# First stage by fourths with the modulation's chunks in front of products, and the heads' score halves in turn in two banks

## The chip, the cores and the metric

The kernel runs on one core of one Trainium2 chip. The metric is the device time of one execution in microseconds (us); lower is better. TensorE (PE) multiplies matrices into PSUM banks, VectorE (DVE), ScalarE (ACT) and GpSimd (POOL) work on elements, and SyncE (SP) issues most of the transfers from HBM. A measurement of this kernel tells about 1% from no change.

## What is computed

The program is two transformer blocks on 256 tokens of width 1024, all in float32. The first block has two layers, each with a modulation from a condition (adaln), differential attention, a pooling mixer, a convolution, an output product and a gated FFN of hidden width 2816. In layer 0 the 256 context tokens go the same way beside the 256 tokens of x, so 512 tokens are worked on; layer 1 needs only x (its keys still come from all 512). The second block (four mixing branches) is not touched. The parts that matter here, from the reference:

```python
def adaln(cond, w_mod, b_mod):
    m = jnp.dot(jax.nn.silu(cond), w_mod) + b_mod
    return jnp.split(m[..., None, :], 6, axis=-1)

# diff_attention, for each block of 128 queries; c = 0, 1 are the two halves of a head
        s = jnp.einsum('bhcqd,bhckd->bhcqk', q_blk, k_all).astype(jnp.float32) * scale
        p = jax.nn.softmax(s, axis=-1)
        a = p[:, :, 0] - lam * p[:, :, 1]
        return jnp.einsum('bhqk,bhkd->bhqd', a.astype(v_all.dtype), v_all)

# first_block, each layer
        sh1, sc1, g1, sh2, sc2, g2 = adaln(c, w_mod[l], b_mod[l])
        h = modulate(rms_norm(x, norm1_g[l]), sh1, sc1)
        q, k, v, up, ca, cb = project_inputs(h, w_in[l], q_norm_g[l], k_norm_g[l])
        attn = diff_attn_post(diff_attention(q, k_all, v_all, lam), subln_g[l], lambda_init)
        pool_o = pool_mixer(up, pool_w[l], pool_scale[l])
        conv_o = conformer_conv(ca, cb, conv_dw_w[l], conv_dw_b[l], conv_ln_g[l], conv_ln_b[l])
        mix = jnp.concatenate([attn, pool_o, conv_o], axis=-1)
        x = x + g1 * jnp.einsum('blm,md->bld', mix, w_out[l])
        x = x + g2 * swiglu(modulate(rms_norm(x, norm2_g[l]), sh2, sc2), w_ffn_in[l], w_ffn_out[l])
```

There are 4 heads, each with two halves of 64 rows for queries and keys and a value width of 128.

## The kernel before

Every large product is taken as three float32r matmuls (`mm3`, lines 359 to 361): both operands are split into a high part and a rest, and high by high, rest by high and high by rest are added in one bank. Features stand as `hH`, `hL` (high and rest). Weights come in chunks of 512 KB (`raw_chunk`, L337) on the SP queue into `wraw` (4 buffers); `weights` casts them on ACT to `whi` (L349) and takes the rest on DVE as `wlo` (L350). PSUM has 8 banks of 512 columns in four pools: `mm` 3, `md` 1, `sc` 2, `aux` 2. A tile scheduler puts each engine's instructions in a fixed order from the order of the code and what each waits for; buffers decide when a load may start.

**First stage.** The x columns come as two 1 MB transfers on ACT's queue, their squares are summed for the norm (L437, L441, L448, L452). The modulation's scale and shift for the first norm come in two groups of 8 chunks, each chunk one row block of 128 by 1024 columns, multiplied by the conditions in four column groups (`modulation`, L513, 256 columns each). When a group's 8 chunks are done, its sums are copied (L518), transposed by TensorE (L520) and added to a bias (L533); then `norm` makes the features of four of the eight row blocks (L495 on DVE, L497 hH on ACT, L498 hL on DVE). `first_norm(0)` runs ahead of any product. The second group's chunks are put between the products of the first three `ab` items (the convolution's inputs, each 8 row blocks by 512 tokens) by `feats` with the table `STEPS`, which gives how many chunks follow which product; the second half of the products waits for the second norm. The fourth item follows alone. The raw chunks share `wraw` and `wmod` buffers (two to one) with the weights of the products.

**What follows in layer 0.** Products for queries and keys, head norm and rope, values, then attention a head at a time among the products of the next head; taps of the convolution on DVE and POOL; the pooling; and last w_out.

**Attention.** A unit is one head and one block of 128 queries (`tt`): 256 keys for the context's blocks (tt < 2), 512 for the others; 16 units in layer 0, 8 in layer 1 in two blocks. `scores` does for each half c: a bank from `sc`, three matmuls on rows 64c to 64c+63, the maximum on DVE (L702), the exponential with its sum on ACT (L704). `values` takes the reciprocal and the difference (L711 to L713, DVE, in place in `e`), transposes it on TensorE (L716), copies it (L718, ACT, `aT`), multiplies by the values (L721), and scales the result (L725, L726). The loop issues the scores of one unit ahead of the values of the present one. `finish` norms a head (L732, L735), transposes it (L738) and splits it. The split pieces live in the pool `hid`, as tiles `hidH` and `hidL` of 512 columns.

**Other places touched.** `layer_scalars` (lam of the layer) and `decay` (a row of the second block) are small chains on ACT and DVE; before, both stand in the first layer's beginning as the scheduler finds room. `single` takes tiles of 512 columns from `hid` in the second block.

## Time and profile before

| | |
|---|---|
| median of 3 runs | 1404.02 us (1397.06 to 1407.89) |
| the profiled execution | 1406.04 us, its span 1404.2 us |
| mean granted clock of TensorE | 0.968 |
| TensorE busy | 1337.7 us, 95% of the span |
| DVE, ACT, POOL busy | 965.5, 602.9, 233.5 us (69%, 43%, 17%) |
| chain that ended last, by engine | PE 83%, DVE 6%, ACT 4%, DMA 3% |
| HBM read | 211.00 MB, 151 GB/s over the span |

A window row gives for a stretch how long each engine worked, how many instructions it had, and the mean granted clock (1.00 is 2.4 GHz, half of it 1.2 GHz). A timeline row gives the start, the length, the engine, the line and operation, what is written and read, and in brackets how long the engine had been idle before and what ended that. Matmuls overlap in the pipeline, so the step from one start to the next is a matmul's price, not the length shown. Times count from the span's start.

### The profile page before, as it was taken

The numbers are of one execution on the slowest core, as the hardware profiler recorded it, in microseconds if no ns is written. First come the engines' busy times: TensorE is split into PE (matmuls) and PEld (weight loads), VectorE is DVE, ScalarE is ACT, GpSimd is POOL, SyncE is SP. The second block draws the span as 40 slices with busy tenths as digits, with TensorE's granted clock in tenths as the row PEclk, the third lists the DMA queues.
The fourth block names the chain that finished last, engine by engine and source line by source line (L and its number), as shares of the span: only waits on it lengthen the run. The fifth ranks groups of instructions, "written<-read, shape, count | busy, mean of one in ns | idle before, by whom it ended". The sixth has DMA issues, their size and how long they took to land.

```text
span 1404.2 us, 22735 instructions
## 1 busy us (share of the span) xinstructions
PE 1337.7 (95%) x8754; PEld 1173.3 (84%) x8754; DVE 965.5 (69%) x1928; ACT 602.9 (43%) x1085; POOL 233.5 (17%) x274
## 2 busy tenths in 40 slices
PE   5899999899999999998988989999999999998999
PEld 2699667798888888888977879999977788998999
DVE  4599766678667767746976655555678677757565
ACT  3333454433222222335344544444565546656443
POOL 0056631310000000013316230000173002000000
PEclk9999999999999999998988889999999999999999
DMA  8424450425444667732321235555564423444553
GB/s 336 178 86 141 161 170 30 151 92 186 157 159 156 196 209 236 237 111 72 109 91 46 81 120 176 195 176 185 168 237 144 152 89 100 149 143 152 186 184 132
DMA packets 61309, 213.53 MB, mean 152 GB/s; under 512 B 6928, under 2 KB 8080, under 8 KB 60944
## 3 DMA queue, kind: packets, MB, share of 16 engines
q1 hardware_dynamic: 60768, 209.91, 44.8%
q10 hardware_dynamic: 432, 2.16, 0.4%
q8 instruction: 69, 1.13, 0.3%
q14 instruction: 40, 0.33, 0.1%
HBM read 211.00 MB, written 1.05 MB: 151 GB/s over the span
## 4 chain that ended last, share of the span: by engine, by line
PE 83%; DVE 6%; ACT 4%; DMA 3%; POOL 2%; issue 2%; SPq 0%; ACTq 0%; POOLq 0%; DVEq 0%
PE ps_mm L359 22%; PE ps_mm L360 22%; PE ps_mm L361 21%; PE ps_sc L359 2%; PE ps_aux L359 2%; DVE wlo L350 2%; PE ps_aux L361 2%; PE ps_aux L360 2%; PE ps_aux L721 1%; PE ps_sc L360 1%; PE ps_sc L361 1%; DVE cacc L820 1%; ACT whi L349 1%; PE ps_md L513 1%; DMA wraw<-in_w_dram 1%
## 5 line engine op out<-in xcount | busy, mean ns | idle before, releaser
L349 ACT CAST whi<-wraw 128x1024 fp32r<-128x1024 f32 (+2 forms) x292 | 300.5, 1033 | 528.6 <-PE ps_mm L360 257.4
L350 DVE TENSOR_TENSOR wlo<-wraw,whi 128x1024 fp32r<-128x1024 f32 (+2 forms) x296 | 356.5, 1206 | 163.4 <-ACT whi L349 160.9
L359 PE MATMUL ps_mm<-hH,whi 128*128 128x256 f32 (+1 forms) x1056 | 344.3, 329 | 11.1 <-ACT hH L497 8.9
L360 PE MATMUL ps_mm<-hL,whi 128*128 128x256 f32 (+1 forms) x1056 | 342.6, 326 | 2.2 <-DVE hL L498 2.2
L361 PE MATMUL ps_mm<-hH,wlo 128*128 128x256 f32 (+1 forms) x1056 | 342.6, 326 | 1.3 <-DVE wlo L350 1.3
L359 PEld LDWEIGHTS ps_mm<-hH,whi 128*128 128x128 f32 x1056 | 204.4, 195 | 32.4 <-ACT hH L497 10.7
L360 PEld LDWEIGHTS ps_mm<-hL,whi 128*128 128x128 f32 x1056 | 204.9, 194 | 19.6 <-DVE hL L498 3.8
L361 PEld LDWEIGHTS ps_mm<-hH,wlo 128*128 128x128 f32 x1056 | 204.6, 194 | 17.7 <-DVE wlo L350 2.5
L359 PE MATMUL ps_mm<-hidH,whi 128*128 128x256 f32 (+1 forms) x683 | 214.1, 316 | 1.7 <-ACT hidH L355 1.7
L360 PE MATMUL ps_mm<-hidL,whi 128*128 128x256 f32 (+1 forms) x683 | 214.4, 315 | 0.0
L361 PE MATMUL ps_mm<-hidH,wlo 128*128 128x256 f32 (+1 forms) x683 | 213.4, 314 | 0.0
L360 PE MATMUL ps_mm<-wlo,hH 128*128 128x256 f32 (+2 forms) x464 | 143.2, 310 | 3.5 <-DVE wlo L350 3.5
L359 PE MATMUL ps_mm<-whi,hH 128*128 128x256 f32 (+2 forms) x464 | 139.9, 310 | 2.1 <-ACT tm L647 1.4
L361 PE MATMUL ps_mm<-whi,hL 128*128 128x256 f32 (+2 forms) x464 | 141.9, 307 | 0.0
L359 PEld LDWEIGHTS ps_mm<-hidH,whi 128*128 128x128 f32 x683 | 129.2, 190 | 10.5 <-ACT hidH L355 1.9
L360 PEld LDWEIGHTS ps_mm<-hidL,whi 128*128 128x128 f32 x683 | 129.8, 190 | 8.9 <-issue 0.5
L361 PEld LDWEIGHTS ps_mm<-hidH,wlo 128*128 128x128 f32 x683 | 129.4, 190 | 8.0
L470 POOL TENSOR_TENSOR squares<-squares,scr 128x256 f32<-128x256 f32 (+1 forms) x28 | 31.6, 1130 | 561.3 <-ACT scr L469 560.8
L580 DVE CUSTOM_DVE_ANT_0 ps_md<-wmod,tm 128x512 f32<-128x512 f32 x160 | 111.5, 697 | 12.4 <-DMA wmod<-in_w_dram 9.7
L848 DVE SCALAR_TENSOR_TENSOR xT<-ps_mm,modv,xT 128x256 f32<-128x256 f32 x116 | 52.5, 479 | 74.1 <-PE ps_mm L361 74.1
L364 POOL TENSOR_TENSOR st<-st,mhalf 128x4 f32<-128x4 f32 (+3 forms) x54 | 65.1, 1209 | 198.8 <-DVE st L632 86.7
L360 PEld LDWEIGHTS ps_mm<-wlo,hH 128*128 128x128 f32 x464 | 88.3, 191 | 9.6 <-DVE wlo L350 5.8
(347 smaller groups left out, 1996.6 us busy)
## 6 DMA issues: line engine op xcount, KB each, us to landing
wraw<-in_w_dram SPq DMA_DIRECT2D x271, 512.0 KB, 3.3
wmod<-in_w_dram SPq DMA_DIRECT2D x85, 512.0 KB, 4.1
wraw<-in_w_dram SPq DMA_DIRECT2D x32, 448.0 KB, 3.2
xT<-in_x_dram ACTq DMA_DIRECT2D x2, 1024.0 KB, 7.0
single<-in_w_dram SPq DMA_DIRECT2D x8, 256.0 KB, 7.5
wraw<-in_w_dram SPq DMA_DIRECT2D x4, 288.0 KB, 3.5
tm<-in_rows_dram SPq DMA_DIRECT2D x4, 256.0 KB, 6.1
out_dram<-scr SPq DMA_DIRECT2D x8, 128.0 KB, 1.7
```

The source lines that it names most:

```text
L349: act.copy(out=hi[:, :m], in_=t[:, :m])
L350: P["split"] = dve.tensor_tensor(lo[:, :m], t[:, :m], hi[:, :m].bitcast(F32), op=ALU.subtract)
L359: pe.matmul(ps, a[0], b[0], start=start, stop=False)
L360: pe.matmul(ps, a[0], b[1], start=False, stop=False)
L361: P["product"] = pe.matmul(ps, a[1], b[0], start=False, stop=stop)
L364: pool.tensor_tensor(t, t, mhalf[:, :n], op=ALU.pow)
L470: eng.tensor_tensor(squares[:, lo:hi], squares[:, lo:hi], q, op=ALU.add)
L513: inst = pe.matmul(ps[g * 32:g * 32 + 32, :256], csil[:, k, :], t[:, g * 256:g * 256 + 256], start=(k == 0), stop=(k == KD - 1), tile_posi ...
L580: dve.tensor_tensor_reduce(bank("md"), t[:, i * 512:i * 512 + 512], crow[2 * j + i], 1.0, 0.0, ALU.mult, ALU.add, sums[j][:, i * KD + d:i ...
L721: pe.matmul(po[:, :128], aT[:, i * 128:i * 128 + 128], v[i][:, h * 128:h * 128 + 128], start=(i == 0), stop=(i == nk // 128 - 1))
L820: dve.scalar_tensor_tensor(av, u[:, j, :n, i:i + 256], colt[:, o + i:o + i + 1], av, op0=ALU.mult, op1=ALU.add)
L848: dve.scalar_tensor_tensor(xT[:, d, r], ps[:, s * 256 - lo:s * 256 - lo + 256], M(l, which, 1 - s)[:, d:d + 1], xT[:, d, r], op0=ALU.mult, ...
```

## The change

1. The modulation of the first norm comes in fourths (`first_modulation`): each fourth gives the scale and shift of two row blocks from four chunks of two row blocks by 512 columns, with matmuls of 128 columns (L515 in the new file). The weights of the ab items come by fourths too, 2 row blocks by the columns of all four items, so that `first_products` fills four banks (3 `mm`, 1 `sc`) a fourth at a time. The raw chunks go into 16 buffers of `hid` and `wmod`. `tc.issue_after` sets the chunks of the next fourth ahead of products.
2. x comes in four transfers of 512 KB at the head of the SP queue.
3. Attention: six score matmuls alternate between the halves, so between rows 0 to 63 and 64 to 127, into both `sc` banks; the maxima and exponentials come after both. Scores run two units ahead, and the product with the values (`values`) one unit late, apart from the transposes (`turned`, the first half of what `values` was).
4. `hid` has tiles of 1024 columns that hold high part and rest (`slot`, `single`); `feats` loses its interleaving; `layer_scalars` is issued after the first stage's products, `decay` late in layer 1's FFN.

```diff
...
@@ -33,13 +33,11 @@
 ROWS_PER_STEP = (3, 1)
 AHEAD = (2, 0)
 POOL_AFTER = ((14, 15), (5, 6))
-STEPS = {1: 1, 2: 1, 3: 1, 4: 1, 5: 1, 6: 1, 7: 1, 8: 1, 11: 9}
 NSCR = 4
 NXS = 3
 
 
-
-MOD_GROUPS = {0: ((4, 5, 0, 1), (6, 7, 2, 3)) + tuple(tuple(range(4 * i, 4 * i + 4)) for i in (2, 4, 3))}
+MOD_GROUPS = {0: tuple(tuple(range(4 * i, 4 * i + 4)) for i in (2, 4, 3))}
 
 
 MIX_PARTS = ((0, 1, 4, 5), (6, 7, 2, 3))
@@ -65,6 +63,12 @@
             cols = np.concatenate([np.arange(c * 256, c * 256 + 256) for c in parts])
             for k in range(8):
                 rows(("mod", l, g, k), "w_mod", (l,), cols, k * 128, 1)
+        if l == 0:
+            for q in range(4):
+                cols = np.arange(q * 256, q * 256 + 256)
+                for k in range(0, 8, 2):
+                    rows(("first", q, k), "w_mod", (l,), np.concatenate([D + cols, cols]), k * 128, 2)
+                rows(("abq", q), "w_in", (l,), np.arange(1792, 2304), q * 256, 2)
         for which in range(6):
             if (l, which) in BY_ROWS:
                 for d in range(8):
...
@@ -296,8 +300,8 @@
     colt = const.tile([128, NCOLS], F32, name="colt")
     dma.dma_start(out=colt[:, :NCOL0], in_=cols[:, :NCOL0])
     xT = const.tile([128, KD, 512], F32, name="xT")
-    for k in range(0, KD, 4):
-        act.dma_start(out=xT[:, k:k + 4], in_=xin.rearrange("p (k t) -> p k t", k=KD)[:, k:k + 4])
+    for k in range(0, KD, 2):
+        dma.dma_start(out=xT[:, k:k + 2], in_=xin.rearrange("p (k t) -> p k t", k=KD)[:, k:k + 2])
     first = const.tile([128, CST0], F32, name="first")
     act.dma_start(out=first, in_=cst[:, 0:CST0])
     ident = first[:, 0:128]
@@ -333,21 +337,28 @@
 
     def raw_chunk(key, pl="wraw"):
         kt, n = PLAN[key][4], len(PLAN[key][3])
-        t = (P["wmod"] if pl == "wmod" else wraw).tile([128, CHUNK], F32, name=pl)
+        t = (wraw if pl == "wraw" else P[pl]).tile([128, CHUNK], F32, name="raw" if pl == "hid" else pl, tag=pl)
         P["load"] = dma.dma_start(out=t[:, :kt * n], in_=w[INDEX[key], :, :kt * n])
...
...
...
@@ -503,6 +502,32 @@
     pool.memset(csil, 0.0)
     act.activation(csil[:, :, 0:2], C("c").rearrange("p (k j) -> p k j", j=2), AF.Silu)
     modv = {l: const.tile([128, 6, KD, 2], F32, name=f"modv{l}") for l in range(DEPTH)}
+
+    def first_modulation(q, pools, p):
+
+        ps = bank(p)
+        for k in range(0, KD, 2):
+            t = raw_chunk(("first", q, k), next(pools))[0]
+            P["first"] = P["load"]
+            for i in range(2):
+                for g in range(4):
+                    o = i * 512 + g * 128
+                    inst = pe.matmul(ps[g * 32:g * 32 + 32, :128], csil[:, k + i, :], t[:, o:o + 128],
+                                     start=(k + i == 0), stop=(k + i == KD - 1), tile_position=(0, g * 32))
+            yield inst
+        cp = P["wk"].tile([128, 256], F32, name="cp")[:, :128]
+        act.copy(out=cp, in_=ps[:, :128])
+        pe.transpose(ps[:, 256:384], cp, ident)
+        got = ps[:, 256:384].rearrange("p (w k c) -> p w k c", w=2, k=2)
+        r = slice(2 * q, 2 * q + 2)
+        for i, which in enumerate((1, 0)):
+            o = COLS["bmod0"][0] + which * 8 + 2 * q
+            dve.tensor_tensor(modv[0][:, which, r], got[:, i, :, 0:2],
+                              colt[:, o:o + 2].unsqueeze(2).to_broadcast([128, 2, 2]), op=ALU.add)
+            if which:
+                dve.scalar_tensor_tensor(scale1[0][:, :, r].rearrange("p j k -> p k j"), modv[0][:, 1, r], 1.0,
+                                         C("n1g")[:, r].unsqueeze(2).to_broadcast([128, 2, 2]),
+                                         op0=ALU.add, op1=ALU.mult)
 
     def modulation(l, group, pools=repeat("wmod"), p="md"):
 
...
@@ -690,23 +716,31 @@
         q0 = qts[0]
 
         def scores(j, tt):
+
             nk = 256 if tt < 2 else 512
             mx, s = st(2), st(2)
+            ps = [bank("sc"), bank("sc")]
+            qs = slice((tt - q0) * 128, (tt - q0) * 128 + 128)
+            for i, (a, b) in enumerate(((0, 0), (0, 1), (1, 0))):
+                for c in range(2):
+                    r = slice(c * 64, c * 64 + 64)
+                    with tc.issue_after(P["product"].ins) if i or c else nullcontext():
+                        P["product"] = pe.matmul(ps[c][:, :nk], qT[j][a][r, qs], kT[j][b][r, :nk], start=i == 0,
+                                                 stop=i == 2)
+            for c in range(2):
+                dve.tensor_reduce(mx[:, c:c + 1], ps[c][:, :nk], axis=AX.X, op=ALU.max, negate=True)
+            return nk, ps, mx, s
+
+        def exps(nk, ps, mx, s):
             e = []
             for c in range(2):
-                r = slice(c * 64, c * 64 + 64)
-                ps = bank("sc")
-                qs = slice((tt - q0) * 128, (tt - q0) * 128 + 128)
-                mm3(ps[:, :nk], (qT[j][0][r, qs], qT[j][1][r, qs]), (kT[j][0][r, :nk], kT[j][1][r, :nk]),
-                    True, True)
-                dve.tensor_reduce(mx[:, c:c + 1], ps[:, :nk], axis=AX.X, op=ALU.max, negate=True)
                 x = P["wk"].tile([128, 512], F32, name="e", bufs=4)
-                act.activation(x[:, :nk], ps[:, :nk], AF.Exp, bias=mx[:, c:c + 1], accum_out=s[:, c:c + 1])
+                act.activation(x[:, :nk], ps[c][:, :nk], AF.Exp, bias=mx[:, c:c + 1], accum_out=s[:, c:c + 1])
                 e.append(x)
             return nk, s, e
 
-        def values(j, tt, ss, nk, s, e):
-            h = h0 + j
+        def turned(j, tt, nk, s, e):
+
             r, cc = st(2), st(1)
             dve.reciprocal(r, s)
             dve.scalar_tensor_tensor(cc, s[:, 0:1], r[:, 1:2], lam, op0=ALU.mult, op1=ALU.mult)
...
@@ -742,15 +780,21 @@
 
         units = [(j, tt) for j in range(len(qT)) for tt in qts]
         sums = {j: st(4) for j in range(len(qT))}
-        ahead = scores(*units[0])
-        for i, (j, tt) in enumerate(units):
-            now = ahead
-            if i + 1 < len(units):
-                ahead = scores(*units[i + 1])
-            values(j, tt, sums[j], *now)
-            if tt == qts[-1]:
-                finish(j, sums[j])
-            each()
+        n = len(units)
+        held = {i: exps(*scores(*units[i])) for i in range(min(2, n))}
+        turn = {}
+        for i in range(n + 1):
+            ahead = scores(*units[i + 2]) if i + 2 < n else None
+            if i:
+                j, tt = units[i - 1]
+                values(j, tt, sums[j], *turn.pop(i - 1))
+                if tt == qts[-1]:
+                    finish(j, sums[j])
+            if i < n:
+                turn[i] = turned(*units[i], *held.pop(i))
+                if ahead:
+                    held[i + 2] = exps(*ahead)
+                each()
 
     def pooled(l, j, h, seqs, mix):
 
@@ -857,14 +901,39 @@
     row = rows_of_rstd(0, 512)
     h = new_h()
 
-    pools = cycle(("wraw", "wraw", "wmod"))
-
-    def first_norm(half):
-
-        yield from modulation(0, half, pools, "sc")
-        norm(h, 0, 512, parts(0, 0, scale1, (0, 1)), range(half * 4, half * 4 + 4), row, True)
-    for _ in first_norm(0):
-        pass
+    def first_products(items):
+
+        pools = iter(("hid",) * 9 + ("wmod",) * 2 + ("hid",) * 5)
+        ps = [bank("mm" if i < 3 else "sc") for i in range(4)]
+        mods = [first_modulation(q, pools, ("md", "sc")[q % 2]) for q in range(4)]
+        ws = {0: weights(("abq", 0))}
+
+        def first_norm(q):
+            for _ in mods[q]:
+                pass
+            norm(h, 0, 512, parts(0, 0, scale1, (0, 1)), range(2 * q, 2 * q + 2), row, True)
+
+        first_norm(0)
+        for q in range(4):
+            for k in range(2):
+                chunk = None
+                if q < 3 and k < 2 - min(q, 1):
+                    with tc.issue_after(P["product"].ins) if q or k else nullcontext():
+                        for _ in range(4 if q else 2):
+                            chunk = next(mods[q + 1])
+                    if q or k:
+                        P["behind"] = P["normed"], P["rest"]
+                        ws[q + 1] = weights(("abq", q + 1))
+                if k and q < 3:
+                    first_norm(q + 1)
+                wH, wL = ws[q]
+                with tc.issue_after(chunk.ins) if chunk else nullcontext():
+                    for (key, _), t in zip(items, ps):
+                        c = slice(key[2] * 128, key[2] * 128 + 128)
+                        mm3(t, (wH[:, k, c], wL[:, k, c]), tuple(x[:, 2 * q + k] for x in h), q + k == 0, q + k == 4)
+        P["behind"] = P["normed"], P["rest"], P["first"]
+        for (_, evac), t in zip(items, ps):
+            evac(t)
 
     def project_rows(l, d_list, make, ks, which, final, first_half, lo, after, each=None):
 
@@ -930,16 +999,17 @@
         n = 512 - lo
         qts = range(2 * seqs[0], 4)
         if not last:
-            queue.extend(modulation(0, g) for g in range(2, 5))
+            queue.extend(modulation(0, g) for g in range(3))
         mix = {}
         u, items = conv_inputs(l, h, seqs)
         if l == 0:
-            feats(items[:3], h, [(0, 512)], first_norm(1))
-            items = items[3:]
-            with tc.issue_after(P["load"].ins):
+            first_products(items)
+            items = []
+            with tc.issue_after(P["first"].ins):
                 R, K = open_consts(False)
                 dma.dma_start(out=colt[:, NCOL0:], in_=cols[:, NCOL0:])
-        layer_scalars(l)
+        with tc.issue_after(P["normed"].ins), tc.issue_after(P["rest"].ins), tc.issue_after(P["product"].ins):
+            layer_scalars(l)
         for it in items:
             feats([it], h, [(lo, 512)])
         acc, taps = conv_taps(l, u, seqs)
@@ -1041,7 +1111,8 @@
                 items = []
                 rows_step(0)
                 if last and f == 10:
-                    decay()
+                    with tc.issue_after(P["high"].ins), tc.issue_after(P["split"].ins):
+                        decay()
             final = t == 2
             if final:
                 h_next = new_h()
...
```

How the rows stand. On TensorE, at the start of the program, before the change (`ps_sc` is the bank of the modulation's sums, `csil` the condition, L437 the sums of squares, L452 the spread of the norm):

```order
L437 MATMUL ps_aux<-ones,scr 128x1
L513 MATMUL ps_sc<-wmod,csil 32x256 x4
L513 MATMUL ps_sc<-wraw,csil 32x256 x8
L513 MATMUL ps_sc<-wmod,csil 32x256 x4
L452 MATMUL ps_aux<-scr,ones 128x512
L513 MATMUL ps_sc<-wraw,csil 32x256 x8
L513 MATMUL ps_sc<-wmod,csil 32x256 x4
L520 MATMUL ps_sc<-first,cp 128x128 x2
L359 MATMUL ps_mm<-hH,whi 128x512
L513 MATMUL ps_sc<-wraw,csil 32x256 x4
L360 MATMUL ps_mm<-hL,whi 128x512
```

In the change the same place on TensorE (L515 is the modulation, L370 to L372 are the three matmuls of a product):

```order
L436 MATMUL ps_aux<-ones,scr 128x1
L515 MATMUL ps_md<-raw,csil 32x128 x24
L451 MATMUL ps_aux<-scr,ones 128x512
L515 MATMUL ps_md<-raw,csil 32x128 x8
L515 MATMUL ps_sc<-raw,csil 32x128 x16
L520 MATMUL ps_md<-first,cp 128x128
L370 MATMUL ps_mm<-hH,whi 128x512 x3
L370 MATMUL ps_sc<-hH,whi 128x512
L371 MATMUL ps_mm<-hL,whi 128x512
L372 MATMUL ps_mm<-hH,wlo 128x512
```

Four chunks stand ahead of the first transpose's sums as before eight of half the rows did, two chunks of the next fourth stand between those and the transpose, and the first products of all four items follow at once.

On TensorE at the first attention block of layer 1, before the change (L716 is the transpose of `e`, `ps_sc` the score banks):

```order
L359 MATMUL ps_sc<-hidH 128x512
L360 MATMUL ps_sc<-hidL,hidH 128x512
L361 MATMUL ps_sc<-hidH,hidL 128x512
L716 MATMUL ps_aux<-first,e 128x128 x4
L359 MATMUL ps_sc<-hidH 128x512
L360 MATMUL ps_sc<-hidL,hidH 128x512
L361 MATMUL ps_sc<-hidH,hidL 128x512
L721 MATMUL ps_aux<-tm,aT 128x128 x4
```

And in the change, the whole block:

```order
L728 MATMUL ps_sc<-hid 128x512 x18
L750 MATMUL ps_aux<-first,e 128x128 x4
L728 MATMUL ps_sc<-hid 128x512
L759 MATMUL ps_aux<-tm,aT 128x128 x4
L728 MATMUL ps_sc<-hid 128x512 x5
L750 MATMUL ps_aux<-first,e 128x128 x4
L759 MATMUL ps_aux<-tm,aT 128x128 x4
```

The scores of three units now stand ahead of the first transpose. DVE's order in the same block of the change (L731 is the maximum, L745 to L747 the reciprocal and the difference, L764 the scaled result):

```order
L731 TENSOR_REDUCE st_6472<-ps_sc 128x1 x2
L731 TENSOR_REDUCE st_6488<-ps_sc 128x1 x2
L731 TENSOR_REDUCE st_6504<-ps_sc 128x1
L745 RECIPROCAL st_6516<-st_6473 128x2
L731 TENSOR_REDUCE st_6504<-ps_sc 128x1
L746 SCALAR_TENSOR_TENSOR st_6517<-st_6473,st_6516,lam 128x1
L747 SCALAR_TENSOR_TENSOR e<-e,st_6517 128x512
```

The difference of the first unit (L747) stands behind both maxima of the third, where before the maxima of at most the next unit stood ahead of it.

## Rows read from the trace of the kernel before

**Rows 1.** Windows: stretch, length, busy PE PEld DVE ACT POOL, PEclk, DMA share, GB/s.
```profile
0.00:66.00 66.00, 44.71 (x250) 27.84 (x251) 31.86 (x87) 24.05 (x43) 3.97 (x16) 0.92 0.70 265
66.00:127.00 61.00, 61.00 (x514) 60.12 (x516) 60.97 (x103) 23.24 (x49) 31.03 (x26) 1.00 0.26 88
127.00:170.00 43.00, 42.27 (x305) 31.43 (x294) 36.36 (x78) 20.04 (x56) 31.01 (x50) 1.00 0.55 196
170.00:222.00 52.00, 48.30 (x299) 29.48 (x298) 32.94 (x81) 27.06 (x79) 14.67 (x17) 0.90 0.38 122
720.00:738.00 18.00, 13.94 (x57) 10.10 (x57) 11.09 (x27) 10.65 (x32) 1.07 (x1) 0.72 0.17 56
759.00:790.00 31.00, 27.94 (x131) 21.04 (x132) 16.72 (x40) 14.61 (x38) 9.78 (x13) 0.75 0.05 19
```

**Rows 2.** Timeline of the first stage, all engines, up to the first product.
```profile
22.65 0.44 PE L520 MATMUL ps_sc<-first,cp 128*128 128x128 f32 x2
...
26.33 1.65 DVE L495 SCALAR_TENSOR_TENSOR tm<-xT,scale,ps_aux 128x256 f32<-128x256 f32 x4
...
27.80 0.79 PE L359 MATMUL ps_mm<-hH,whi 128*128 128x512 f32 x1 [4.71 <-ACT hH L497]
```

**Rows 3.** Timeline of TensorE among the first products.
```profile
32.56 0.63 PE L359 MATMUL ps_mm<-hH,whi 128*128 128x512 f32 x1
32.99 0.63 PE L360 MATMUL ps_mm<-hL,whi 128*128 128x512 f32 x1
...
37.85 0.39 PE L359 MATMUL ps_mm<-hH,whi 128*128 128x512 f32 x1
...
38.30 0.39 PE L361 MATMUL ps_mm<-hH,wlo 128*128 128x512 f32 x1
38.62 0.64 PE L513 MATMUL ps_sc<-wraw,csil 128*32 128x256 f32 x8
...
39.52 0.39 PE L360 MATMUL ps_mm<-hL,whi 128*128 128x512 f32 x1
...
47.29 0.73 PE L359 MATMUL ps_mm<-hH,whi 128*128 128x512 f32 x2 [0.76 <-ACT hH L497]
```

**Rows 4.** Waits of the SP queue in 0:60 (us in total, times, longest us).
```profile
SPq L337 <- PE ps_sc L513: 12.7, 10, 4.8
```

**Rows 5.** Timeline of TensorE at score matmuls, in three places.
```profile
132.49 0.28 PE L361 MATMUL ps_mm<-whi,hL 128*128 128x256 f32 x1
132.70 0.49 PE L359 MATMUL ps_sc<-hidH 64*128 64x512 f32 x1
...
133.59 0.38 PE L359 MATMUL ps_mm<-whi,hH 128*128 128x256 f32 x1
...
210.68 0.50 PE L359 MATMUL ps_sc<-hidH 64*128 64x512 f32 x1
...
213.93 0.50 PE L359 MATMUL ps_sc<-hidH 64*128 64x512 f32 x1
...
717.83 0.50 PE L359 MATMUL ps_sc<-hidH 64*128 64x512 f32 x2
718.17 0.40 PE L360 MATMUL ps_sc<-hidL,hidH 64*128 64x512 f32 x2
```

**Rows 6.** Groups by line: count, busy us, mean ns, idle before (127:222; loads: whole).
```profile
L702 DVE TENSOR_REDUCE st<-ps_sc 128x1 f32<-128x512 f32 x16 | 11.0, 687 | 10.0 <-PE ps_sc L361 10.0
L713 DVE SCALAR_TENSOR_TENSOR e<-e,st 128x512 f32<-128x512 f32 x7 | 6.3, 896 | 0.1
L704 ACT ACTIVATE e<-ps_sc,st 128x512 f32<-128x512 f32 x16 | 11.1, 694 | 4.6 <-DVE st L702 2.9 <-DVE st L711 1.6
L704 ACT ACTIVATION_READ_ACCUMULATOR e<-ps_sc,st 128x1 f32 x30 | 6.1, 202 | 0.0
L704 ACT ACT_TABLE_LOAD x2 | 2.6, 1283 | 0.0
```

**Rows 7.** Waits of TensorE in 717:790 (us in total, times, longest us).
```profile
PE ps_sc L359 <- ACT e L704: 3.2, 2, 2.4
```

59 lines of the change are left out of this document (31 added, 28 removed).

## The prediction

> **What bounds the kernel now.** I read the windows of the stages first, then the timeline of each stage that the change touches, then the waits of the engines there. The windows [rows 1] say that TensorE sets the time nearly everywhere, and that the touched stages are where it does not. In 0:66 it works for 44.71 of 66 us, at a mean granted clock of 0.92. In 66:127 and 127:170 it is full (61.00 of 61, 42.27 of 43), and DVE is just as full in 66:127 (60.97). In 170:222 it has 48.30 of 52 at clock 0.90. The two attention blocks of layer 1, 720:738 and 759:790, are the loosest: 13.94 of 18 and 27.94 of 31, at clocks 0.72 and 0.75. So a microsecond that the first stage gives back should reach the end if what follows is full, and a matmul saved in 66:170 is worth its own time. In 170:222 and in layer 1's blocks the chain scores, maximum, exponential, transpose counts.
>
> In the first stage the timeline [rows 2, 3] shows the first product at 27.80, behind an idle 4.71 us for hH. The chunks of the second half of the modulation stand between products, and TensorE waits again at 47.29 when the second half's features come. The SP queue waits for buffers ten times, 12.7 us, until an L513 has read one [rows 4]. In 0:66 the DMA brings 265 GB/s at a share of 0.70 [rows 1]; that is 265/0.70 = 379 GB/s while it flows.
>
> **The first stage.** The bytes are the same, 12 MB of x, modulation and ab weights. Only their order changes, and 16 chunk buffers instead of a few keep the queue from waiting.
>
> *First product.* Ahead of the first transpose on TensorE stand 2 MB of x, 0.5 MB of ab weights, the 2 MB of fourth 0 and, by the order of TensorE shown above, the first 1 MB of fourth 1: 5.5 MB, 5.5/0.379 = 14.5 us, and 3 us that I allow for the start of the transfers: 17.5. The last chunk's matmuls and the copy of the sums bring the transpose to about 19.3. Before, from transpose (22.65) to product (27.80) took 5.15 us, of which 3.7 passed until the first features' tm at 26.33, since late weights' wlo stood ahead of it on DVE [rows 2]. In the change the ab weights of fourth 0 come first and are long split, so only about 2.5 us remain: first product 21.8, between 20 and 23.5.
>
> *Products.* 4 banks by 8 k by 3 is 96 matmuls. At full clock they start 0.225 us apart (37.85 to 38.30 is two) [rows 3], 22.1 us with 0.23 each. At the low clock they start 0.43 apart (32.56 to 32.99). I let 16 of them run so, 16 x 0.20 = 3.2 us; the bounds are 6 (1.2) and 24 (4.8).
>
> *Chunks between products.* From 38.30 to 39.52 there lie two product steps and one chunk of 8 matmuls of 256 columns: 1.22 - 0.45 = 0.77 us [rows 3]. Ten of the twelve chunks of fourths 1 to 3 stand behind the first product. Their matmuls are as many but half as wide; no row shows that width, so a chunk lies between 0.4 (half) and 1.0 (0.77 with a wait for data); I take 0.7 because the switches and the starts stay: 7 us.
>
> *Seams.* Before, one seam cost 0.76 us for hH at 47.29 [rows 3] and more for hL. Now there are three, 1.0 each: 3 us, between 1.5 and 6.
>
> 21.8 + 22.1 + 3.2 + 7 + 3 = 57.1 us, where the stage now ends 0.4 ahead of the window's end, at 65.6: **8.5 us gained**, with bounds, not all at once on one side, of 3 to 13. That DVE is full from 66 on [rows 1] does not take the gain away at once: its queue there is fed by the evacuations of these products and moves with them.
>
> *layer_scalars* and *decay* are costed at nothing. decay is a table load and some DVE operations on a few columns. It leaves the first stage (DVE 31.86 of 66 busy) [rows 1] for layer 1's FFN, where TensorE has products to cover it. A table load is 1.28 us [rows 6]; with as much again for DVE, 2.5 us is its price without that cover.
>
> **The attention of layer 0.** One half alone among products takes from 132.49 to 133.59, less one product step of 0.12: 0.98 us for three matmuls of 512, of which the product and score switches are about 0.3 [rows 5]. Two halves cost about 2.0. In the change six matmuls stand next to each other with alternating rows. That two of them can run side by side is seen at 717.83: a pair L359 and a pair L360 start only 0.34 us apart, the time of one [rows 5]. If that holds for all three pairs a unit costs about 1.1, if not 6 x 0.23 + 0.4 = 1.8. It saves 0.2 to 0.9 for 512 keys and half that for 256. Eight of the sixteen units lie in 127:170, where TensorE is full: at most 4 x 0.9 + 4 x 0.45 = 5.4, at least 1.2; **I take 4**, since the trace shows the pair.
>
> In 170:222 the units are not hidden. There they come 3.25 us apart now (210.68, 213.93) [rows 5]. In the change both banks are taken at once, so scores (0.9), the first maximum (0.69) and both exponentials (2 x 0.89 with their accumulator reads) follow each other until both banks are free [rows 6]: 3.4, with handovers 3.6. That is 0.35 more for each of some five such units; with less matmul time in between I book **+1.5**, between -4 and +5.
>
> **Layer 1.** Here the whole loop is exposed. In 720:738 TensorE waits 3.2 us in two pieces for an exponential to free a score bank [rows 7]. In the change three units' scores (18 matmuls) stand ahead of the first transpose, and DVE has the third unit's maximum in front of the first unit's L747, as its order shows. Four units at the 3.6 from above are 14.4, and behind the last exponential come its L747 (0.90) [rows 6], transpose, copy and values with handovers, some 4 in all: about 18.5 us, as now. The second block has up products and transposes between; two units ahead should fill part of its 3 us of waiting: **-2 for both**, between -7 and +3. The order shows two more table loads than before on ACT, 2 x 1.28 us [rows 6], beside products; they and the slightly shifted second half are booked at 0, within 3 either way.
>
> **Sum.** -8.5 - 4 + 1.5 - 2 = -13. Against the profiled execution (1406.0) that is 1393, against the median of the three runs (1404.0) 1391: **1392**.
>
> **A rule weighed.** The pair at 717.83 speaks for side by side work [rows 5]. The Trainium skill, page "TensorEngine Tiling (Array Packing)", section "PSUM Bottleneck", says that tiling makes TensorE faster but not the emptying of PSUM, which may then be the limit. The 3.2 us of TensorE waiting for an exponential [rows 7] agree with it. By that rule the 4 us in layer 0 would be lost too, and the sum would be -9; if the loop grew as well it is the third rival.
>
> **Rivals.**
> 1. *Both parts work fully.* Chunks cost 0.5, products run at full clock (stage ends near 52, -13), pairs overlap everywhere (-8 in layer 0, -4 in layer 1): -25, 1380. For it speaks the pair at 717.83; against it that the clock falls whenever TensorE idles in a stage (0.72 in 720:738) [rows 1].
> 2. *The first stage's gain is swallowed.* DVE is as full as TensorE in 66:127 [rows 1]. If what it does there (wlo, taps) is bound by loads or by work that cannot start earlier, the 8.5 us turn into waits there, and only the attention is left: -3, 1402. Against it: in 66:127 the DMA runs at a share of 0.26 only, so loads do not hold it.
> 3. *The attention loop gets longer*, which ends on the other side. Both banks are taken together, and L747 (0.90) stands behind the maxima of the unit two ahead. If each exposed unit pays both, 0.35 + 0.90 = 1.25 us, the seven of layer 0's last stretch and eight of layer 1 cost 19; with -8.5 of the first stage that is +10: 1416. It decides against the change from 8.5/15 = 0.6 us a unit. Against it: DVE has slack there: ahead of the maxima of 512 keys it idles 10.0 us in all, waiting for scores [rows 6].
> 4. *The alternating matmuls do not overlap*: the scheduler's order is right but a pair takes twice one. Then layer 0 saves only the switches, 1.2: -10, 1396, inside the forecast's own spread.
>
> **How the numbers follow.** The forecast with rival 4 (1384 to 1399) has 0.52, rival 1 0.20, rival 2 0.15, rival 3 0.13. The range 1376 to 1408 leaves out about half of rival 3 and a quarter of rival 1. A measurement tells about 1% here, 14 us, so faster means below 1390 and slower above 1418. Below 1390 lie rival 1 and 0.24 of the forecast: 0.44. Above 1418 lies the far half of rival 3: 0.07. The rest is 0.49.
>
> **What would show it.** In the changed trace: the first product near 21.8, the SP queue without waits for L515, the last ab product near 57, a chunk between products at 0.7. A unit's six score matmuls should take about 1.1 us, with both banks' first matmuls starting within 0.1. Layer 0's w_out should begin about 11 us earlier than 222. The block at 720 should stay near 18 us. The prediction is wrong if the stage ends after 62, if the time from the stage's end to w_out grows by more than 3 us, or if the blocks of layer 1 take over 50 us together.

## The result and the profile after

The changed kernel takes 1414.31 us (median of 13 runs, 1408.32 to 1420.43) beside 1406.18 us of the kernel before (13 runs, 1397.06 to 1412.52): a ratio of 1.0058 with an interval of 1.0038 to 1.0079. It is 8 us slower, where 12 to 14 us less was forecast, and it lies above the range. The direction is that of the third rival.

The windows of the changed kernel answer to [rows 1] (stretch, length, busy PE, PEld, DVE, ACT, POOL, then PEclk, DMA share, GB/s):

```profile
0.00:66.00 66.00, 51.21 (x479) 42.33 (x480) 39.59 (x84) 28.04 (x51) 8.83 (x18) 1.00 0.74 282
66.00:127.00 61.00, 61.00 (x507) 58.62 (x506) 60.84 (x102) 21.88 (x50) 33.57 (x30) 1.00 0.30 99
127.00:170.00 43.00, 38.23 (x223) 25.37 (x222) 26.39 (x62) 19.69 (x52) 27.16 (x45) 0.84 0.42 139
170.00:222.00 52.00, 42.64 (x287) 25.98 (x286) 30.36 (x82) 23.47 (x71) 10.03 (x13) 0.87 0.39 135
720.00:738.00 18.00, 11.50 (x39) 7.22 (x36) 8.28 (x19) 6.46 (x19) 0.00 (x0) 0.50 0.00 1
759.00:790.00 31.00, 18.89 (x96) 12.83 (x96) 17.64 (x37) 12.68 (x33) 10.72 (x15) 0.84 0.19 62
```

In the first window TensorE now works 51.21 us at full clock instead of 44.71 at 0.92. In all windows with attention it works less than before, and in 127:222 and 720:738 at a lower clock: 0.84, 0.87 and 0.50 instead of 1.00, 0.90 and 0.72.

Where the time went is read from the starts of the same instruction in the profiled executions. A profile shows one execution, and executions of one kernel differ: of the ten of experiment 1 below the profiled one was the slowest, 1407.08 us at a mean granted clock of 0.965, beside a median of 1400.3 and a fastest of 1394.18 at 0.974. The columns are the start of the first query and key product, of the first w_out product of layer 0, of the first scores of layer 1 (block 1), of the products that go on behind block 1, of the first scores of block 2, and of layer 1's w_out:

| kernel | q, k | w_out 0 | block 1 | goes on | block 2 | w_out 1 |
|---|---|---|---|---|---|---|
| before | 65.80 | 222.05 | 717.83 | 736.22 | 759.19 | 788.37 |
| after | 53.56 | 219.30 | 713.28 | 738.58 | 761.28 | 796.36 |
| difference | -12.24 | -2.75 | -4.55 | +2.36 | +2.09 | +7.99 |

Some of these starts, before and then after:

```profile
65.80 0.40 PE L359 MATMUL ps_mm<-whi,hH 128*128 128x256 f32 x2
...
222.05 1.42 PE L359 MATMUL ps_mm<-hidH,whi 128*128 128x512 f32 x1
...
736.22 0.39 PE L359 MATMUL ps_mm<-whi,hH 128*128 128x256 f32 x1 [1.39 <-ACT tm L647]
```
```profile
53.56 0.39 PE L370 MATMUL ps_mm<-whi,hH 128*128 128x256 f32 x1
...
219.30 1.27 PE L370 MATMUL ps_mm<-hid,whi 128*128 128x512 f32 x1
...
713.28 0.73 PE L728 MATMUL ps_sc<-hid 64*128 64x512 f32 x4 [0.74 <-ACT hid L366]
...
738.58 0.58 PE L370 MATMUL ps_mm<-whi,hH 128*128 128x256 f32 x1 [1.14 <-ACT tm L672]
```

So the first stage gained 12.2 us. Between there and w_out the changed kernel lost 9.5 of them, and each block of layer 1 lost again: 25.30 us instead of 18.39, and 35.08 instead of 29.18. Between layer 0's w_out and block 1 it lost some 2 us and won some 4, as is told below.

The timeline of the first stage after (start, length, engine, line and operation, and in brackets the idle time before with what ended it), to be held against [rows 2, 3]:

```profile
20.83 0.33 PE L520 MATMUL ps_md<-first,cp 128*128 128x128 f32 x1
23.08 0.96 PE L370 MATMUL ps_mm<-hH,whi 128*128 128x512 f32 x3 [1.92 <-ACT hH L496]
...
25.82 0.39 PE L372 MATMUL ps_sc<-hH,wlo 128*128 128x512 f32 x1
26.14 1.08 PE L515 MATMUL ps_sc<-raw,csil 128*32 128x128 f32 x32
27.16 0.50 PE L370 MATMUL ps_mm<-hH,whi 128*128 128x512 f32 x1
...
47.45 0.96 PE L370 MATMUL ps_mm<-hH,whi 128*128 128x512 f32 x3 [0.99 <-ACT hH L496]
...
52.93 0.39 PE L372 MATMUL ps_sc<-hH,wlo 128*128 128x512 f32 x1
```

The products run from 23.08 to 52.93, all at the full clock. TensorE waits 1.92 us for hH ahead of the first, 0.26 and 0.99 at two of the seams. Of the SP queue's waits for an L513 [rows 4] nothing is left.

Now the ring that makes the attention longer. This is block 1 of layer 1 after the change, all engines, from the second unit's last exponential to its transposes:

```profile
722.20 0.20 ACT L738 ACTIVATION_READ_ACCUMULATOR e<-ps_sc,st 128x1 f32 x1
...
723.74 0.69 DVE L731 TENSOR_REDUCE st<-ps_sc 128x1 f32<-128x512 f32 x1 [2.23 <-PE ps_sc L728]
...
725.25 0.75 DVE L747 SCALAR_TENSOR_TENSOR e<-e,st 128x512 f32<-128x512 f32 x1
726.10 0.69 ACT L738 ACTIVATE e<-ps_sc,st 128x512 f32<-128x512 f32 x1 [3.71 <-DVE e L747]
726.15 1.09 PE L750 MATMUL ps_aux<-first,e 128*128 128x128 f32 x4 [2.06 <-DVE e L747]
...
727.91 2.08 PE L759 MATMUL ps_aux<-tm,aT 128*128 128x128 f32 x8
...
729.92 1.65 PE L728 MATMUL ps_sc<-hid 64*128 64x512 f32 x5
...
731.19 0.69 DVE L731 TENSOR_REDUCE st<-ps_sc 128x1 f32<-128x512 f32 x1 [0.32 <-PE ps_sc L728]
...
732.70 0.75 DVE L747 SCALAR_TENSOR_TENSOR e<-e,st 128x512 f32<-128x512 f32 x1
...
733.60 1.09 PE L750 MATMUL ps_aux<-first,e 128*128 128x128 f32 x4 [2.03 <-DVE st L745]
```

Both exponentials of the second unit are done at 722.40, so its difference L747 could run then. It runs at 732.70, because on DVE it stands behind the maxima of the fourth unit (731.19). Those wait for the fourth unit's scores. The first of these waited for a score bank, which an exponential of the third unit had to empty; the other five (729.92) then stood behind the first unit's values (727.91) on TensorE. That exponential (726.10) came 3.71 us after ACT's last work and ran when L747 of the first unit was done: there are four buffers for `e`, two units' worth, and until L747 and the transposes have read the first unit's they are full. Its own maximum was ready at 724.43, so the buffer accounts for the last 1.6 us of that wait. So the chain is a ring: difference, exponential of the unit two further, scores of the one behind it, its maxima, next difference. Transposes come 7.45 us apart (726.15, 733.60); before, they came 4.48 apart:

```profile
726.75 1.11 PE L716 MATMUL ps_aux<-first,e 128*128 128x128 f32 x4
...
731.23 1.06 PE L716 MATMUL ps_aux<-first,e 128*128 128x128 f32 x4
```

How long exponentials wait in all until a difference is done (us in total, times, longest us) shows the buffer's link in layer 0 (130:245) and in layer 1 (690:810) of the changed kernel:

```profile
ACT e L738 <- DVE e L747: 11.9, 5, 2.9
ACT e L738 <- DVE e L747: 7.5, 2, 3.8
```

Before, in 130:245 (in 690:810 there is none):

```profile
ACT e L704 <- DVE e L713: 0.4, 1, 0.4
```

### The profile page after: what moved, and what is told of

Read it like the earlier page. It is cut to its first block, busy times and chain, and to the rows that moved or that the text cites. A ratio compares the mean times of both kernels' runs of the same rounds, so it can differ in the third digit from the quotient of the medians.

```text
span 1410.5 us, 23000 instructions
## 1 busy us (share of the span) xinstructions
PE 1328.5 (94%) x8882; PEld 1170.8 (83%) x8882; DVE 962.1 (68%) x1932; ACT 606.9 (43%) x1089; POOL 235.5 (17%) x274
## 4 chain that ended last, share of the span: by engine, by line
PE 83%; DVE 7%; POOL 4%; ACT 3%; issue 2%; DMA 1%; SPq 0%; ACTq 0%; POOLq 0%; DVEq 0%
PE ps_mm L370 22%; PE ps_mm L371 22%; PE ps_mm L372 21%; PE ps_aux L370 2%; PE ps_aux L372 2%; PE ps_aux L371 2%; DVE cacc L864 2%; PE ps_aux L759 2%; DVE wlo L361 1%; PE ps_sc L728 1%; POOL st L375 1%; PE ps_sc L370 1%; PE ps_aux L1513 1%; PE ps_sc L372 1%; PE ps_sc L371 1%
## 5 line engine op out<-in xcount | busy, mean ns | idle before, releaser
L370 PE MATMUL ps_mm<-hH,whi 128*128 128x256 f32 (+1 forms) x1056 | 341.5, 327 | 6.6 <-ACT hH L496 6.6
L372 PE MATMUL ps_mm<-hH,wlo 128*128 128x256 f32 (+1 forms) x1056 | 340.0, 323 | 0.0
L370 PEld LDWEIGHTS ps_mm<-hH,whi 128*128 128x128 f32 x1056 | 202.4, 193 | 26.5 <-ACT hH L496 8.6
L370 PE MATMUL ps_mm<-hid,whi 128*128 128x256 f32 (+1 forms) x683 | 214.3, 316 | 2.9 <-ACT hid L366 2.9
L372 PEld LDWEIGHTS ps_mm<-hH,wlo 128*128 128x128 f32 x1056 | 202.6, 192 | 15.2 <-issue 0.6
L371 PE MATMUL ps_mm<-hid,whi 128*128 128x256 f32 (+1 forms) x683 | 213.9, 314 | 0.6 <-DVE hid L367 0.6
L372 PE MATMUL ps_mm<-hid,wlo 128*128 128x256 f32 (+1 forms) x683 | 213.2, 314 | 0.0
L370 PE MATMUL ps_mm<-whi,hH 128*128 128x256 f32 (+2 forms) x464 | 140.9, 312 | 1.7 <-ACT tm L672 1.1
L372 PE MATMUL ps_mm<-whi,hL 128*128 128x256 f32 (+2 forms) x464 | 142.3, 309 | 0.0
L370 PEld LDWEIGHTS ps_mm<-hid,whi 128*128 128x128 f32 x683 | 129.3, 190 | 11.8 <-ACT hid L366 3.3
L371 PEld LDWEIGHTS ps_mm<-hid,whi 128*128 128x128 f32 x683 | 129.6, 190 | 9.6 <-DVE hid L367 1.1
L372 PEld LDWEIGHTS ps_mm<-hid,wlo 128*128 128x128 f32 x683 | 129.1, 189 | 7.9
```

The costliest lines, as they stand in the source:

```text
L370: pe.matmul(ps, a[0], b[0], start=start, stop=False)
L371: pe.matmul(ps, a[0], b[1], start=False, stop=False)
L372: P["product"] = pe.matmul(ps, a[1], b[0], start=False, stop=stop)
```

## The experiments

All runs are compared with the kernel before on the same chip. The stage times come from the same two instructions as in the table above, in one profiled execution of each run. Expectations that put block 1 of the changed kernel near 28 or 29 us mean the block that the table has at 25.30.

### 1. The attention of before in the changed kernel

```diff
-            ps = [bank("sc"), bank("sc")]
-            for i, (a, b) in enumerate(((0, 0), (0, 1), (1, 0))):
...
+            for c in range(2):
+                ps = bank("sc")
+                mm3(ps[:, :nk], (qT[j][0][r, qs], qT[j][1][r, qs]), (kT[j][0][r, :nk], kT[j][1][r, :nk]),
+                    True, True)
+                dve.tensor_reduce(mx[:, c:c + 1], ps[:, :nk], axis=AX.X, op=ALU.max, negate=True)
...
-        held = {i: exps(*scores(*units[i])) for i in range(min(2, n))}
+        ahead = scores(*units[0])
...
+                ahead = scores(*units[i + 1])
+            values(j, tt, sums[j], *turned(j, tt, *now))
```

> The changed kernel with the attention code of before (halves one after the other, scores one unit ahead, values at once); first stage, merged hid tiles and moved decay stay. Theory A (the loss is in the attention): the 12.2 us gained by the end of the first stage stay to the end, about 1393, block 1 of layer 1 back to 18.4 us. Theory B (the loss comes from the other edits: hid tiles, layer_scalars, decay, shifted order): it stays at 1405 or more.

1400.3 us, ratio 0.9955 (0.9931 to 0.9979). Block 1 is back at 18.90 us, so its loss is the attention's. Block 2 is not: 32.98, between 29.18 before and 35.08 after. By the median only 6 to 7 us of the first stage's gain are left. In the profiled execution none are left at w_out: q, k products start at 53.95, w_out at 223.49, 169.5 us later, where it was 156.25 before. In between the granted clock is low there: windows of 15 us.

```profile
145.00:160.00 15.00, 15.00 (x77) 10.43 (x75) 7.97 (x20) 7.60 (x26) 7.54 (x17) 0.63 0.44 143
190.00:205.00 15.00, 15.00 (x64) 8.24 (x64) 5.69 (x13) 4.17 (x13) 0.00 (x0) 0.51 0.37 121
```

TensorE is busy for the whole of both windows, at 0.63 and 0.51 of full speed; before, it had 1.00 and 0.77 there. Theory A as put (the gain stays to the end) is only half right, and in layer 0 the attention is not the only cause of the loss: in this execution the kernel loses there with the attention of before.

### 2. One unit ahead, alternating halves kept

```diff
-        held = {i: exps(*scores(*units[i])) for i in range(min(2, n))}
-            ahead = scores(*units[i + 2]) if i + 2 < n else None
+        ahead = exps(*scores(*units[0]))
+            if i + 1 < len(units):
+                ahead = exps(*scores(*units[i + 1]))
+            values(j, tt, sums[j], *turned(j, tt, *now))
```

> The changed kernel with its six alternating score matmuls, but the loop of before: scores one unit ahead, values at once. On DVE the first unit's L747 then stands behind the maxima of the second unit and no longer behind those of the third. Theory order (L747 and with it the next exponentials wait in a ring for maxima two units ahead): block 1 goes from about 29 us back to 18 to 20, the total to about 1394 to 1398. Theory banks (taking both score banks for one unit is what lengthens the loop): block 1 stays near 27 or more and the total above 1408.

1398.68 us, ratio 0.9947 (0.9925 to 0.9968). Block 1 takes 19.82 us, q, k to w_out 155.85 (after: 165.74, before: 156.25). DVE's rows in block 1 show the order:

```profile
707.79 1.29 DVE L731 TENSOR_REDUCE st<-ps_sc 128x1 f32<-128x512 f32 x2 [2.20 <-PE ps_sc L728]
709.44 0.75 DVE L747 SCALAR_TENSOR_TENSOR e<-e,st 128x512 f32<-128x512 f32 x1
711.31 1.29 DVE L731 TENSOR_REDUCE st<-ps_sc 128x1 f32<-128x512 f32 x2 [1.11 <-PE ps_sc L728]
712.96 0.75 DVE L747 SCALAR_TENSOR_TENSOR e<-e,st 128x512 f32<-128x512 f32 x1
```

The first L747 stands behind the second unit's maxima instead of the third's; it comes 3.0 us behind the first unit's exponentials (706.47) instead of 6.4 (718.90 and 725.25 after). Transposes are 3.92 us apart (711.59, 715.51). Of the exponentials' waits for L747 this is left in 130:245, and nothing in 690:810:

```profile
ACT e L738 <- DVE e L747: 2.5, 1, 2.5
```

Taking both score banks for a unit did not make block 1 long again: the theory of the banks falls.

### 3. Two ahead, but the halves in turn

```diff
-            for i, (a, b) in enumerate(((0, 0), (0, 1), (1, 0))):
...
+            for c in range(2):
+                r = slice(c * 64, c * 64 + 64)
+                ps.append(bank("sc"))
+                mm3(ps[c][:, :nk], (qT[j][0][r, qs], qT[j][1][r, qs]), (kT[j][0][r, :nk], kT[j][1][r, :nk]),
+                    True, True)
+                dve.tensor_reduce(mx[:, c:c + 1], ps[c][:, :nk], axis=AX.X, op=ALU.max, negate=True)
```

> The changed kernel with its loop (two units ahead, values one late), but each half's three score matmuls together, c0 then c1, each followed by its maximum. Theory order: the ring stays, block 1 stays at 26 us or more, total 1410 to 1420. Theory banks: block 1 near 18 us, total about 1395.

1404.74 us, ratio 0.9991 (0.9966 to 1.0017), block 1 19.94 us, block 2 33.89. Both expectations miss: it lies between. With the halves apart the second half's maximum of the unit ahead stands behind L747 and not ahead of it, so half of what L747 waits for is gone; the exponentials wait 4.0 us for the difference in 130:245 and 4.8 in 690:810, instead of 11.9 and 7.5. The order on DVE is thus a joint effect of two ahead and of both maxima in one piece.

### 4. and 6. Six e buffers, and the control

```diff
-                x = P["wk"].tile([128, 512], F32, name="e", bufs=4)
+                x = P["wk"].tile([128, 512], F32, name="e", bufs=6)
-    open_pools(stack1, dict(mm=3, md=1, sc=2, aux=2, cst=1, hid=9, tm=12, wk=1, wmod=2))
+    open_pools(stack1, dict(mm=3, md=1, sc=2, aux=2, cst=1, hid=8, tm=12, wk=1, wmod=2))
-        pools = iter(("hid",) * 9 + ("wmod",) * 2 + ("hid",) * 5)
+        pools = iter(("hid",) * 8 + ("wmod",) * 2 + ("hid",) * 6)
```

The control has the hid lines alone.

> The changed kernel with 6 buffers for the exponentials e instead of 4 (and 8 hid tiles instead of 9 to make room). The third unit's exponentials then need not wait until the first unit's L747 and transposes have freed theirs. Theory order with its ring through the e buffers: the ring is cut, block 1 falls from 29 us to about 20 to 23, the total to about 1400 to 1406. Theory banks: no change, about 1413.

> The changed kernel with 8 hid tiles instead of 9 and still 4 e buffers: the control for the run with 6 e buffers. Theory order: as the changed kernel, about 1414, block 1 near 29 us. If it is near 1398 the hid tiles, not the e buffers, brought the gain.

With six buffers 1398.19 us, ratio 0.9941 (0.991 to 0.9972); the control 1415.85, ratio 1.0068 (1.0041 to 1.0095), as the changed kernel. So the e buffers bring 18 us. Block 1 goes from 25.29 (control) to 22.48, block 2 from 36.61 to 29.70, q, k to w_out from 166.77 to 159.21; the control's profiled execution took 1420.83, 5 us above its median. In layer 1 the exponentials no longer wait for L747, and the transposes are 3.66 us apart (716.18, 719.84); in 130:245 this is left of the control's 12.7 us:

```profile
ACT e L738 <- DVE e L747: 2.4, 3, 1.2
```

The order on DVE is still two ahead, so the first L747 comes late: at 713.89, where the first scores started at 702.32. That is why block 1 stays longer than with one unit ahead.

### 5. The changed attention alone

In the kernel before, the function `attention` is replaced by the changed one; nothing else.

> The kernel before with the changed attention alone (alternating halves, two ahead, values late); first stage, hid tiles and decay as before. Theory order (the ring makes the attention longer, whatever comes before it): slower than before by 8 to 16 us, block 1 of layer 1 near 28 us where before has 18. Theory timing (the attention only suffers because it starts 12 us earlier): within 4 us of before.

1426.12 us, ratio 1.0137 (1.0094 to 1.0181): 19 us slower. Block 1 takes 25.29 us, as in the changed kernel, block 2 34.76, and q, k to w_out 163.45, 7.2 us more than before. It needs no earlier start to be slow; that theory falls. 19 - 12 for the first stage is 7, and the change measured +8, so by this sum the two parts add. By experiment 1 they don't: there the rest of the change brings 7 us and not 12, and the attention costs 14 and not 19.

### 7. One ahead and six e buffers

> One unit ahead and values at once, with alternating halves and 6 e buffers (8 hid tiles). Theory order: cutting the ring once is enough, so this is as the two single cuts, 1394 to 1399. Should both cuts add, 1388 to 1392.

The edits of experiments 2 and 4 together. 1386.03 us (1384.26 to 1391.29), ratio 0.9858 (0.9802 to 0.9914): faster than both kernels, by 1.4% and 2%. Most of the two gains adds: 15.6 us (experiment 2) and 17.7 (experiment 4 beside its control) are 33 together, and 28 came. That is below both expected ranges, and the ring does not explain it: by the ring alone one cut is enough. Block 1 is 19.65, block 2 31.98, q, k to w_out 154.19, little less than in experiment 2. What is left of the exponentials' waits for L747 there, 2.5 us, is gone here; the rest of the 12.7 us between experiments 2 and 7 stays unexplained.

### 8. Waits filled with extra matmuls

```diff
             pt = bank("aux")
+            for i in range(6 if l else 0):
+                pe.matmul(pt, kT[j][0][:, 0:128], kT[j][0][:, 0:512], start=True, stop=True)
             for i in range(nk // 128):
                 pe.transpose(pt[:, i * 128:i * 128 + 128], e[0][:, i * 128:i * 128 + 128], ident)
```

> The changed kernel with six extra 512-column matmuls ahead of each unit's transposes in layer 1, into the bank that the transposes then overwrite; 8 units x 6 x 0.23 = 11 us of extra work at full clock, part of it in places where TensorE waits. Theory clock (half of the loss in block 1 is the low clock): the granted clock in block 1 goes from 0.50 to above 0.8 and the block gets shorter, 29 to about 24, total 1408 to 1412. Theory order alone: the clock may rise, but the block stays at 29 or grows by the extra work, total 1414 to 1424.

1428.47 us, ratio 1.0159 (1.0113 to 1.0206). The two windows are those of block 1, of this run and of the changed kernel:

```profile
717.70:745.40 27.70, 18.33 (x60) 11.70 (x60) 13.26 (x29) 8.64 (x26) 0.00 (x0) 0.60 0.12 38
```
```profile
713.30:738.60 25.30, 14.73 (x49) 8.92 (x49) 13.26 (x29) 8.71 (x26) 0.00 (x1) 0.54 0.12 42
```

Against expectation the fill hardly raised the clock (0.60 beside 0.54); it lengthened the block by 2.4 us. So it does not tell what a full clock would be worth there; it shows only that filling these waits costs time.

### 9. and 10. Which of the two: two ahead, or the late values

In 9 the look two units ahead stays:

```diff
-                values(j, tt, sums[j], *turn.pop(i - 1))
...
-                turn[i] = turned(*units[i], *held.pop(i))
+            values(j, tt, sums[j], *turned(j, tt, *held.pop(i)))
```

In 10 the late values stay:

```diff
-        held = {i: exps(*scores(*units[i])) for i in range(min(2, n))}
+        held = {0: exps(*scores(*units[0]))}
...
-            ahead = scores(*units[i + 2]) if i + 2 < n else None
+            if i + 1 < n:
+                held[i + 1] = exps(*scores(*units[i + 1]))
```

> The changed kernel with scores two units ahead, but the values at once behind their transposes. DVE's order still has the third unit's maxima ahead of the first L747. Theory order (two ahead is what makes the ring): block 1 stays at 25 us, total 1410 to 1416. Theory late values (holding the values back one unit is what costs): block 1 below 21 us and 1396 to 1400.

> The changed kernel with scores one unit ahead, values still one unit late. Theory order: block 1 about 20 us as with one ahead and values at once, total 1396 to 1401. Theory late values: stays at 1410 or more.

Two ahead with values at once: 1413.11 us, ratio 1.0062 (1.0041 to 1.0083), block 1 25.28. One ahead with late values: 1398.43, ratio 0.9944 (0.9924 to 0.9964), block 1 19.83. With experiment 2 and the changed kernel these are all four combinations: two ahead costs 14 to 16 us, the late values nothing that can be measured.

### 11. The worth of the alternation

> One ahead, values at once, 6 e buffers, but each half's three matmuls together. Beside the run with alternating halves (1386.0) it gives the worth of the alternation by itself. If the alternation saves its 4 to 8 us of TensorE time in layer 0 and little in layer 1, this is 1390 to 1396; if it is hidden, 1385 to 1388.

As experiment 7, but each half's three matmuls together. 1390.46 us, ratio 0.9895 (0.9865 to 0.9925), beside 1386.03: by the medians the alternation by itself is worth some 4 us, but the four runs of each overlap (1389.18 to 1391.6, and 1384.26 to 1391.29), so this is not clear of the noise. In the profiled executions q, k to w_out is 157.61 instead of 154.19, block 1 18.84 instead of 19.65: there it pays in layer 0, where TensorE has products to do, and not in layer 1.

### 12. The best attention with the first stage of before

> The kernel before with the best attention so far (alternating, one ahead, values at once, 6 e buffers, 8 hid tiles) and the first stage of before. Theory: the first stage's 12 us and the attention add, so this is 12 to 16 us above 1386.0 with the moved decay and scalars: 1398 to 1402. If the first stage's gain were swallowed later, it is 1386 to 1391.

1405.35 us, ratio 1.0002 (0.998 to 1.0024), 19 us above experiment 7. So with this attention the rest of the change keeps all that the first stage gains, and brings more than the 12 to 16 us expected; what the other 7 us are was not separated. The attention of experiment 7 in the kernel before gains nothing that can be measured: q, k start at 64.04 there, w_out at 220.98.

## Why the prediction was wrong

**First stage: right in mechanism, too small in size.** It said 8.5 us; it is 12.2. The first product came at 23.08 instead of 21.8, behind a transpose at 20.83 instead of 19.3 and then 2.25 us where 2.5 were reckoned. What was over-priced: the low clock (3.2 us; all products run at full clock), and the seams (3 us; they are 0.26 and 0.99 behind the first product). One pair of chunks takes from the start of the product at 25.82 to that at 27.16 1.34 us less one step of 0.23, about 0.55 a chunk; 0.7 was taken. The reading behind that price was wrong: a chunk's matmuls are not as many but half as wide, they are twice as many (x32 for two chunks, where it was x8 for one) and half as wide. That TensorE works only 51.21 of 66 us there at a clock of 1.00 also goes against the first rival's objection that the clock falls whenever TensorE idles in a stage. The second rival, that the full DVE behind it swallows this, is refuted: DVE works 60.84 of 61 us in 66:127 after as well, and with one unit ahead (experiment 2) w_out starts at 209.59, 12.5 us earlier than before. Its -3 was mis-added besides: -4 + 1.5 - 2 is -4.5.

**Scores in layer 0: the matmuls as forecast, the time not clearly.** The pair at 717.83 [rows 5] was read rightly. Six matmuls of 512 columns at full clock:

```profile
208.39 0.96 PE L728 MATMUL ps_sc<-hid 64*128 64x512 f32 x6
209.29 0.44 PE L545 MATMUL ps_md<-first,cp 128*128 128x128 f32 x2
```

From 208.39 to 209.29 there are 0.90 us, less than the 1.1 taken. The 4 us it was to bring agree with experiment 11 beside 7, which is not clear of the noise; put into the kernel before, the whole attention of experiment 7 brings nothing that can be measured (experiment 12). In the changed kernel nothing of them shows, because q, k to w_out grew by 9.5 us.

**The loop: the step that failed.** The prediction booked +1.5 us for layer 0's exposed units and -2 for layer 1's blocks. With the changed attention alone, layer 0 took 7.2 us more up to w_out, block 1 6.9 and block 2 5.6. Two of the three signs of being wrong that the prediction named came: from the stage's end to w_out 9.5 us were added, and the blocks of layer 1 take 60.4 us together.

The working of block 1 multiplied a pitch of 3.6 us, which is scores, maximum and two exponentials until both banks are free, by four units. That pitch is right from the second to the third unit (scores at 718.29 and 721.78, 3.49 apart), but not from there to the fourth (most of its scores start at 729.92). The sum saw that L747 stands behind the third unit's maxima and that both banks are taken; it did not ask which buffer the third unit's exponentials write into. With four `e` buffers and two units held they write into the first unit's, so L747, which had been put behind the third unit's work, is also what that work needs. That the order makes a wait and the buffer closes it into a ring is what was missing.

Of block 1's 6.9 us, more buffers give back 2.8 (25.29 to 22.48), one unit ahead 5.5 (25.30 to 19.82): the order is the larger part. The working also ran all four units through to their values; in both traces only two are transposed in the block, and the products go on when ACT comes to their copies (L647 before, L672 after the change).

The third rival named the place (L747 behind the maxima two ahead), with 1.25 us a unit; measured, a unit in block 1 cost 3.0 us more (7.45 beside 4.48). It was given 0.13. That its sum of 19 us for the loop is what experiment 5 measures is luck, since the price of a unit was not right; and the range left out more of it than the half that the text says, since its time, 1416, lies outside.

**Layer 1's beginning.** It was booked at nothing. Before, TensorE waits there 2.2 us for ACT (in 630:690):

```profile
PE ps_mm L359 <- ACT scr L800: 2.2, 1, 2.2
```

After, that wait is gone, and the lead grows there from 1.9 us (the same product starts at 657.8 before, at 655.9 after) to 5.9 (672.1 and 666.2). The moved layer_scalars or decay are not needed for this: in experiment 5, where neither is moved, the stretch from layer 1's first product to its first query and key product takes 15.0 us (660.15 to 675.10), in the changed kernel 13.9 (649.42 to 663.34), before 18.3 (650.95 to 669.22). Nor is the changed attention needed: experiment 1, without it, has 14.4 (650.81 to 665.16). The cause stays open. Some 2 us had been lost in w_out of layer 0: the last units' values and the last head's features come inside it, and TensorE waits 1.2 and 0.6 us there for `hid` (L366, L367), which it did not before.

**The rule weighed.** The Trainium skill, page "TensorEngine Tiling (Array Packing)", section "PSUM Bottleneck", pointed at emptying the banks. By the rule alone the scores' saving would be lost; experiment 11 speaks against that with 4 us that are not clear of the noise. What grew was not the emptying (a maximum takes 0.69 us and an exponential 0.69, before as after), but the wait until the engine that empties gets to it.

**The clock.** In 130:220 the granted clock is 0.85 after and 0.95 before, in block 1 0.54 and 0.72. Behind the wait of 2.06 us in block 1 the values (L759, 2.08 us for 8) and scores (1.65 for 5) run at half speed; at the full clock the same take 1.16 and 0.96 (in block 2, at 795.12 and 768.00). How much of the loss is the clock's own was not separated; experiment 8 was meant to and did not.

## What to carry over

When a loop is made to run further ahead, count for each buffer in it how many units it holds, and follow for each engine's order whether what is put in front of an older step needs a buffer that this older step frees. Two such links close a ring, and cutting either one pays: here 16 us for the order and 18 for the buffers, and cutting both gave 1386.0 us. An engine's idle time ahead of an operation ("DVE idles 10 us waiting for scores") is no slack when the operation that stands behind it is what the waiting depends on.

## What was not expected of the hardware

In the profiled execution of experiment 1, with the old attention, the first stage's 12 us were all given back in layer 0: TensorE was busy in the profile for the whole of 145:160 and 190:205, at a granted clock of 0.63 and 0.51, where before had 1.00 and 0.77. With six `e` buffers, one unit ahead and the halves also in turn (experiment 11) the clock stayed at 1.00 in 145:160, and q, k to w_out took 157.61 us instead of 169.5. So a stretch without a gap in the profile can still run at half speed. Ahead of it TensorE waited 1.94 us for `hid` up to 142.32, and the scores at 145.84 ran at half speed (0.39 us from one matmul of 256 columns to the next, at full speed 0.22). Whether that wait is the cause stays open.
